# A two-layer diffusion backbone on one Trainium2 core: Q ahead of K, three conditioning sums beside layer 0's experts, and a router on x without its norm

## The chip, the cores and the metric

The kernel runs on one core of one Trainium2 chip. The metric is device time of one execution, in microseconds. The core has TensorE (PE, matmuls; PEld in the profile is its weight load), VectorE (DVE), ScalarE (ACT), GpSimd (POOL) and SyncE (SP), which here only issues DMAs. All weights are float32 and come from HBM once, through one queue of SP.

## What is computed

Two layers on 256 latent tokens and 256 context tokens of width 1024. Cut to what matters here:

```python
mod = silu_c @ ada_w[layer] + ada_b[layer]            # 6 vectors of 1024 for each layer
shift1, scale1, gate1, shift2, scale2, gate2 = split(mod, 6)
h = rmsnorm(x) * (1 + scale1) + shift1
if layer == 0:
    q, k, v, xb, gb = split(h @ w_in)                  # k, v, xb also of the context
    attn = neighbourhood_attention(q, k, v)            # q and k normed by head
    xc = conv4(xb)                                     # depthwise, 4 taps
    y = rglru_forward(xc) + rglru_backward(xc)         # two gated linear scans
    mix = concat(attn, gelu(gb) * y) @ w_out
else:
    mix = real(fft2(h by groups of 256 channels)) @ fnet_w_out
x = x + gate1 * mix
h2 = rmsnorm(x) * (1 + scale2) + shift2
scores = sigmoid(h2 @ router_w)                        # 16 experts, 1 of 4 groups, top 2 in it
x = x + gate2 * sum_over_experts(gates * expert(h2))   # silu(h2 @ Wg) * (h2 @ Wu) @ Wd
```

## The kernel before

**The stream.** Every weight matrix comes in loads of 1 MB into one of 16 slots of SBUF. `Stream` keeps a list of the loads in the order in which they will be used; `pump` issues the next one on SP's queue when a slot is free, and `give`, called by `done` and `used`, frees a slot when its last reader is through. The list is built ahead: the projections of layer 0 in the order of the letters in `ORDER` ("a" is the next ada piece of `ADA`, the letters Q, G, V, o, p the projections, B the attention's bias), then `FILL0`, the eight pairs of layer 0's experts (g, u and d of a pair, four loads each), the two halves of fnet's weights, `GAP` and `FILL1`, then layer 1's experts. An ada piece (l, j) is 512 columns of `ada_w[l]` and fills two slots.

**The ada pieces.** `ada_te` does one piece on TensorE: 64 matmuls with the slot as the stationary operand and the conditioning vector as the moving one, in the tile gv; ACT copies the result (gvr), TensorE turns it, DVE adds the bias into `modc`. In layer 0's front the pieces of `ADA` are interleaved with the projections by the tables `W_K`, `W_Q`, `W_G`, `W_V`; the three pieces of `GAP` run between the last expert of layer 0 and the DFT, `FILL1[0]` in the router of layer 1.

**The front.** Each projection (`gemm`) goes over 8 rows of its weight matrix; a row is split into a high and a low part (ACT makes the high part, DVE or POOL the low one, as the strings `EK`, `EQ`, `EG`, `EV` say: v is DVE, g is POOL) and used in three matmuls (`mm3`, L384 to L386). The order is K, Q, G, V, then attention and `w_out`. Beside them run tasks in pieces: the convolution and the gates of the recurrence beside K, its first scan beside Q and G, the head norms `hk` and `hq` in G and V, the second recurrence beside V. TensorE's order is written out by hand there; that of the other engines is set by a scheduler.

**The norm and the router.** `normed` adds the gated mix to x (gm, xt), sums the squares on ACT and scales x by its norm into xn on DVE. `moe` transposes xn (tp), applies scale and shift to it while it leaves PSUM (h2T), multiplies with the router weights as the stationary operand (lg, four groups of 32 rows), copies that (lr) and folds it with a second product (pick). The selection follows as a chain of small DVE operations (sel, cmp, ..., oh, S); ACT makes xh and POOL xl, the two parts of xn for the gather (xg).

**The experts.** For a pair of experts `up` runs g and u (the gathered tokens stationary, 64 rows for each expert), `transposed_act` at, `down` dn in two halves of 512 columns; the scatter ya of a pair runs inside the next one. The first halves of g, u and dn read two slots, the second halves the other two. In layer 0 the result stays in PSUM and the second norm reads it.

## Time and profile before

| | us |
|---|---|
| median of 3 runs | 792.27 (791.53 to 793.74) |
| profiled execution | 794.38 |
| its span in the trace | 792.6 |
| layer 0's projections, scans, attention | 0 to 248 |
| layer 0's router | 248 to 275.3 |
| layer 0's experts | 275.3 to 490.6 |
| norm, ada pieces, DFT | 490.6 to 523.2 |
| fnet's projection | 523.2 to 546.9 |
| layer 1's router | 546.9 to 571.7 |
| layer 1's experts | 571.7 to 792.6 |

TensorE is busy 89% of the span, DVE 35%, ACT 30%, POOL 16%. The stages are read from TensorE's timeline by the first matmul of each kind. The views that the prediction uses are the slices of the page, the list of waits (for each operation what it waited for last), timelines (one line for a run of like instructions, with the idle time before it in brackets), and groups of instructions by line of the code.

### The profile page before, as it was taken

To read this page: it belongs to the slowest core of one execution; us is meant where nothing else is said; L and a number is where in the kernel's file an instruction comes from. 1 tells how busy PE (TensorE), PEld (TensorE's weight loads), DVE (VectorE), ACT (ScalarE), POOL (GpSimd) and SP (SyncE) were. 2 spreads that over 40 slices of the span, in tenths; PEclk is the share of its full clock that TensorE was granted. 3 is DMA by queue.
4 is the path that set the end of the run, shared out by engine and by line. 5 is a ranking of instruction groups with operands and counts; after the bars stand their busy time and mean duration, and the time that the engine had idled before them with its cause. 6 is when DMAs were issued, how large, how long until landed. Compare 5 with 4: busy or idle time off the path is not lost. (4 is left out here: it accounts for less than half of the span.)

```text
span 792.6 us, 11546 instructions
## 1 busy us (share of the span) xinstructions
PE 708.8 (89%) x4707; PEld 388.6 (49%) x4707; DVE 277.2 (35%) x551; ACT 241.6 (30%) x432; POOL 129.6 (16%) x109
## 2 busy tenths in 40 slices
PE   3999979994997799799999997899699799999996
PEld 2677659563775633343444333667434343344334
DVE  3556388166654511111121104344511111121115
ACT  6233955963665310100110003254310110111001
POOL 1243271363321200000000001032201000000002
PEclk8899998996999899999999999899799999999998
DMA  8989756485656789999999999999299999999995
GB/s 275 356 329 385 311 222 264 167 304 228 265 196 253 296 358 421 416 405 421 421 420 423 418 421 422 420 420 351 112 374 422 417 411 421 421 420 420 423 399 170
DMA packets 53793, 277.41 MB, mean 350 GB/s; under 512 B 4898, under 2 KB 20832, under 8 KB 22496
## 3 DMA queue, kind: packets, MB, share of 16 engines
q1 hardware_dynamic: 53008, 275.95, 87.0%
q8 instruction: 41, 0.67, 0.3%
q10 hardware_dynamic: 720, 0.59, 0.2%
q14 instruction: 24, 0.20, 0.1%
HBM read 275.47 MB, written 1.05 MB: 349 GB/s over the span
## 5 line engine op out<-in xcount | busy, mean ns | idle before, releaser
L1042 PE MATMUL g<-slot,xg 128*64 128x512 f32 x512 | 116.2, 608 | 7.9 <-PEq L1145 7.9
L1079 PE MATMUL dn<-slot,aT 128*64 128x512 f32 (+1 forms) x544 | 114.1, 571 | 3.2 <-DVE aT L1063 3.2
L1042 PE MATMUL u<-slot,xg 128*64 128x512 f32 x512 | 113.0, 592 | 0.0
L372 POOL TENSOR_TENSOR wp<-slot,wp 128x512 fp32r<-128x512 f32 x50 | 68.8, 1385 | 161.6 <-ACT wp L371 161.5
L1042 PEld LDWEIGHTS g<-slot,xg 128*64 128x64 f32 x512 | 38.3, 140 | 81.7 <-issue 80.8
L1048 DVE TENSOR_TENSOR act<-act,u 128x512 f32<-128x512 f32 x16 | 11.0, 687 | 192.1 <-PE u L1042 192.1
L1042 PEld LDWEIGHTS u<-slot,xg 128*64 128x64 f32 x512 | 38.0, 137 | 72.2 <-issue 71.7
L1079 PEld LDWEIGHTS dn<-slot,aT 128*64 128x64 f32 x544 | 37.5, 137 | 68.5 <-issue 60.2
L331 PE MATMUL gv<-slot,sc 128*32 128x128 f32 x1536 | 58.2, 293 | 12.1 <-DMA slot<-in_ada_w_dram 7.7
L1081 ACT ACTIVATE yH<-dn,gcol 128x512 fp32r<-128x512 f32 (+1 forms) x34 | 22.5, 662 | 130.5 <-PE dn L1079 125.3
L997 ACT ACTIVATE xg<-xg,modc,a 128x256 f32<-128x256 f32 x32 | 18.0, 564 | 136.5 <-PE xg L988 136.5
L331 PEld LDWEIGHTS gv<-slot,sc 128*32 128x32 f32 x1536 | 47.8, 118 | 24.0 <-issue 13.0
L999 POOL TENSOR_TENSOR SG<-S,gates 128x512 f32<-128x512 f32 x8 | 8.4, 1044 | 310.5 <-PE st L1051 302.1
L1082 DVE SCALAR_TENSOR_TENSOR yL<-dn,gcol,yH 128x512 fp32r<-128x512 f32 (+1 forms) x34 | 24.4, 719 | 93.6 <-ACT yH L1081 85.4
L371 ACT ACTIVATE wp<-slot 128x512 fp32r<-128x512 f32 x72 | 44.3, 627 | 38.0 <-PE qp L386 11.6
L1047 ACT ACTIVATE act<-g 128x512 f32<-128x512 f32 x16 | 9.6, 597 | 121.4 <-PE g L1042 121.4
L988 PE MATMUL xg<-S,xh 128*128 128x256 f32 x128 | 28.4, 306 | 3.8 <-DVE S L976 2.6
L995 DVE TENSOR_SCALAR xg<-xg,a,modc 128x256 f32<-128x256 f32 x32 | 17.4, 543 | 29.4 <-ACT xg L997 29.4
L988 PE MATMUL xg<-S,xl 128*128 128x256 f32 x128 | 27.4, 298 | 0.0
L1019 PE MATMUL ya<-yH,ST 128*128 128x512 f32 x60 | 26.2, 437 | 0.5 <-ACT yH L1081 0.2
L988 PEld LDWEIGHTS xg<-S,xh 128*128 128x128 f32 x128 | 22.1, 209 | 5.5 <-issue 3.2
L1019 PE MATMUL ya<-yL,ST 128*128 128x512 f32 x60 | 23.9, 399 | 0.9 <-DVE yL L1082 0.9
(252 smaller groups left out, 1047.0 us busy)
## 6 DMA issues: line engine op xcount, KB each, us to landing
slot<-in_moe_g_dram SPq DMA_DIRECT2D x64, 1024.0 KB, 13.5
slot<-in_moe_u_dram SPq DMA_DIRECT2D x64, 1024.0 KB, 15.2
slot<-in_moe_d_dram SPq DMA_DIRECT2D x60, 1024.0 KB, 16.3
slot<-in_ada_w_dram SPq DMA_DIRECT2D x40, 1024.0 KB, 8.3
slot<-in_w_in_dram SPq DMA_DIRECT2D x8, 1024.0 KB, 7.2
slot<-in_ada_w_dram SPq DMA_DIRECT2D x12, 512.0 KB, 9.0
slot<-in_w_out_dram SPq DMA_DIRECT2D x4, 1024.0 KB, 6.3
slot<-in_fnet_w_dram SPq DMA_DIRECT2D x4, 1024.0 KB, 19.8
```

The lines of the kernel that those rows point to most:

```text
L331: te.matmul(out=p[32 * q:32 * q + 32, 0:128], lhsT=sc32[:, k, :], rhs=W[:, k, c:c + 128], start=(k == 0), stop=(k == 7))
L371: ac.activation(dst_h, src, AF.Copy)
L372: eng.tensor_tensor(dst_l, src, dst_h.bitcast(F32), op=ALU.subtract)
L988: at_xg[0] = te.matmul(out=p[:, i * 256:(i + 1) * 256], lhsT=xx[:, tb, k * 128:(k + 1) * 128], rhs=S[:, tb * 256:(tb + 1) * 256], start=(n ...
L995: ve.tensor_scalar(xg[:, k], pv, a2[:, k:k + 1], b2[:, k:k + 1], op0=ALU.mult, op1=ALU.add)
L997: ac.activation(xg[:, k], pv, AF.Identity, scale=a2[:, k:k + 1], bias=b2[:, k:k + 1])
L1019: te.matmul(out=yacc[tb * 2 + h], lhsT=ST[:, tb * 128:(tb + 1) * 128], rhs=y[:, h * 512:(h + 1) * 512], start=(p == 0 and n == 0), stop=(n ...
L1042: te.matmul(out=q[half(i), :], lhsT=xg[:, k, half(i0 + i)], rhs=W[i][:, k], start=(k == 0), stop=(k == 7))
L1048: ve.tensor_tensor(act, act, gu[1], op=ALU.mult)
L1079: te.matmul(out=dn[half(i), :], lhsT=aT[:, fc * 128 + 64 * i:fc * 128 + 64 * i + 64], rhs=W[i][:, fc, c], start=(fc == 0), stop=(fc == 3))
L1081: ac.activation(yH[:, c], dn, AF.Copy, scale=gcol)
L1082: ve.scalar_tensor_tensor(yL[:, c], dn, gcol, yH[:, c].bitcast(F32), op0=ALU.mult, op1=ALU.subtract)
```

## The change

1. Q comes before K in the stream and on TensorE. All of Q's low parts are made on POOL (`EQ`). The convolution now runs beside Q, the gates of the first recurrence and the start of its scan beside K, the rest of the scan beside G, where both head norms begin; the tables are set accordingly. In the attention the recurrence's part of the concatenation and the projection's first step come two steps later.
2. `GAP` is gone. Its three pieces, now `BESIDE`, are loaded behind d of pairs 4, 5 and 6 of layer 0 and summed by `ada_inplace`: eight DVE operations of 128x512 multiply the rows of the piece by the conditioning vector and sum them in place, then four matmuls with one moving column sum over the partitions.
3. `FILL1`'s two pieces run in the second place of layer 1's router, behind the logits, not in the first.
4. `normed` becomes `add_mix`: it gives only the reciprocal r of the norm. The router transposes x itself, its weights carry the scale (w2), the shift becomes a row of biases (crow) from a matmul with ones, and r comes in on DVE behind the product (sc). xh takes r as its scale on ACT; xl is made on DVE, not on POOL. The DFT reads x, and its table carries r (dr).
5. `warm(n)` issues n matmuls of 352 columns whose result nobody reads: 5 in layer 1's router, 3 behind rk in both routers, 8 behind layer 0's experts.

```diff
-FILL1 = [[(1, 10), (1, 11)], [], []]
-GAP = [(1, j) for j in (7, 8, 9)]
-ORDER = 'aaaQaBaaGaaVaapoa'
-EQ = 'vgvgvgvg'
+FILL1 = [[], [(1, 10), (1, 11)], []]
+BESIDE = [(1, j) for j in (7, 8, 9)]
+ORDER = 'aaKaaBaGaaVaaapoa'
+EQ = 'gggggggg'
...
+            if l == 0 and n == "d" and p - 4 in range(len(BESIDE)):
+                r.append(ada_item(*BESIDE[p - 4]))
...
+    def ada_inplace(l, j):
+        W = st.get(("a", l, j))
+        r = W[:, 0]
+        ve.tensor_scalar(r, r, sc32[:, 0, 0:1], None, op0=ALU.mult)
+        for k in range(1, 8):
+            ve.scalar_tensor_tensor(r, W[:, k], sc32[:, k, 0:1], r, op0=ALU.mult, op1=ALU.add)
+        W.done(1)
+        yield
+        p = wps("gv")
+        for q in range(4):
+            te.matmul(out=p[:, q:q + 1], lhsT=r[:, q * 128:(q + 1) * 128], rhs=ones[:, 0:1], start=True, stop=True)
+        c4 = slice(4 * j, 4 * j + 4)
+        ve.tensor_tensor(modc[l][:, c4], p[:, 0:4], ada_b[l][:, c4], op=ALU.add)
+        W.done(0)
+        yield
...
     for n, _ in enumerate(gemm(st.get(("win", WQ)), lambda w, k: rows(qp, w, 2, k), EQ)):
-        scan[0](int(W_Q[1][n]))
-        side(int(W_Q[0][n]))
+        conv(1)
+        side(int(W_Q[n]))
...
+    for n, _ in enumerate(gemm(st.get(("win", WK)), lambda w, k: rows(kp, w, 4, k), EK)):
+        gates[0](int(W_K[1][n]))
+        scan[0](int(W_K[2][n]))
+        side(int(W_K[0][n]))
...
+    def warm(n):
+        p = gps("warm")
+        for _ in range(n):
+            te.matmul(out=p[:, 0:352], lhsT=ones, rhs=cst, start=True, stop=True)
...
+        r = tn([128, 2], "rr", bufs=2)
+        ve.tensor_tensor(r, ss[:, :, 0], ss[:, :, 1], op=ALU.add)
+        ac.activation(r, r, AF.Sqrt, scale=1.0 / D, bias=eps)
+        last = ve.reciprocal(r, r)
...
+        for k in range(8):
+            for tb in range(2):
+                at = te.matmul(out=lv[:, tb], lhsT=xT[:, k, tb * 128:(tb + 1) * 128], rhs=w2[:, k],
+                               start=(k == 0 and tb == 0), stop=(k == 7 and tb == 1))
...
-            gp.tensor_tensor(xl[:, tb], xn[:, tb], xh[:, tb].bitcast(F32), op=ALU.subtract)
+            ac.activation(xh[:, tb], xt[:, tb], AF.Copy, scale=r[:, tb:tb + 1])
+            ve.scalar_tensor_tensor(xl[:, tb], xt[:, tb], r[:, tb:tb + 1], xh[:, tb].bitcast(F32),
+                                    op0=ALU.mult, op1=ALU.subtract)
+        sc = tn([128, 2, NE], "sc")
+        for tb in range(2):
+            ve.scalar_tensor_tensor(sc[:, tb], lv[:, tb], r[:, tb:tb + 1], crow, op0=ALU.mult, op1=ALU.add)
...
                 u = up(p, xg)
+                if l == 0 and p - 5 in range(len(BESIDE)):
+                    next(beside)
...
                 pend = down(u[0], act_t, *u[2:])
+                if l == 0 and p - 4 in range(len(BESIDE)):
+                    beside = ada_inplace(*BESIDE[p - 4])
+                    next(beside)
...
-    fins = [ada_pe(*a, ps_=(gps, wps, wps)[i]) for i, a in enumerate(GAP)]
-    xn, last = normed(yacc, gate, a8("xn", [128, 2, D]))
+    warm(8)
+    r, _ = add_mix(yacc, gate)
+        ve.tensor_scalar(dr[:, tb], dt[:, tb], r[:, tb:tb + 1], None, op0=ALU.mult)
```

What the change moves on the engines, from the order of instructions that each program gives its engines. SP's queue in layer 0's experts, before: the last d loads of pair 6, the DFT's table, the first g load of pair 7.

```order
L128 DMA slot_6632<-in_moe_d_dram 128x2048 [waits DMAHW1_49,PE_49]
L128 DMA slot_6642<-in_moe_d_dram 128x2048 [waits DMAHW2_49,PE_49]
L128 DMA slot_6644<-in_moe_d_dram 128x2048 [waits DMAHW3_49,PE_49]
L123 DMA dft<-in_dft_dram 128x514 [waits DMASW3_49,DMASW7_49,DVE_49,DMAHW4_49,Activation_49,Pool_49]
L128 DMA slot_6710<-in_moe_g_dram 128x2048 [waits DMAHW5_49,PE_49]
```

The same place after: the last d loads of pair 6, then the third ada piece, then g of pair 7.

```order
L129 DMA slot_6738<-in_moe_d_dram 128x2048 [waits DMAHW7_49,PE_49]
L129 DMA slot_6740<-in_moe_d_dram 128x2048 [waits DMAHW0_49,PE_49]
L129 DMA slot_6753<-in_ada_w_dram 128x2048 [waits DMAHW1_49,PE_49]
L129 DMA slot_6755<-in_ada_w_dram 128x2048 [waits DMAHW2_49,PE_49]
L129 DMA slot_6765<-in_moe_g_dram 128x2048 [waits DMAHW3_49,DVE_49]
```

The table went ahead of the last two d loads, and two ada loads came in ahead of pair 7, as two each did behind d of pairs 4 and 5; the load behind a piece waits for DVE.

TensorE at the end of layer 0's experts, before: the last rows of dn of pair 7, the scatter ya, and the first ada piece of the gap (gv).

```order
L1079 MATMUL dn<-slot_6777,aT 64x512
L1019 MATMUL ya<-yH,ST 128x512 [waits Activation_49]
L1019 MATMUL ya<-yL,ST 128x512 [waits DVE_49]
L1019 MATMUL ya<-yH,ST 128x512 [waits Activation_49]
L1019 MATMUL ya<-yL,ST 128x512 [waits DVE_49]
L1019 MATMUL ya<-yH,ST 128x512
L1019 MATMUL ya<-yL,ST 128x512
L1019 MATMUL ya<-yH,ST 128x512
L1019 MATMUL ya<-yL,ST 128x512
L331 MATMUL gv<-slot_6846,sc_127 32x128 [waits DMAHW5_49,PE_49]
L331 MATMUL gv<-slot_6846,sc_127 32x128 x15
L331 MATMUL gv<-slot_6848,sc_127 32x128 [waits DMAHW6_49]
```

After: the middle of dn of pair 7, whose second half reads the last two d loads, to the first row of the scatter.

```order
L1122 MATMUL dn<-slot_6833,aT 64x512
L892 MATMUL warm<-cst 128x352 [waits PE_49]
L1122 MATMUL dn<-slot_6863,aT 64x512 [waits DMAHW5_49]
L892 MATMUL warm<-cst 128x352 x4
L1122 MATMUL dn<-slot_6865,aT 64x512 [waits DMAHW6_49]
L1122 MATMUL dn<-slot_6863,aT 64x512
L1122 MATMUL dn<-slot_6865,aT 64x512
L1122 MATMUL dn<-slot_6863,aT 64x512
L1122 MATMUL dn<-slot_6865,aT 64x512
L1122 MATMUL dn<-slot_6863,aT 64x512
L1122 MATMUL dn<-slot_6865,aT 64x512
L1062 MATMUL ya<-yH,ST 128x512 [waits Activation_49]
```

Five warming matmuls stand inside dn, four of them ahead of the first row that needs the very last load. Three more stand among the scatter's rows, and the DFT follows straight behind it, with no ada piece.

DVE in the front, before, around the evacuation of Q (qr<-qp): Q's last and G's first splits (wp), then the head norms (hs, kq).

```order
L372 TENSOR_TENSOR wp<-slot_945,wp 128x512 [waits DMAHW4_49,Activation_49]
L372 TENSOR_TENSOR wp<-slot_945,wp 128x512 [waits Activation_49]
L594 COPY qr<-qp 128x512 [waits PE_49]
L605 TENSOR_REDUCE hs<-sq 128x8 [waits Activation_49] x5
L372 TENSOR_TENSOR wp<-slot_963,wp 128x512 [waits DMAHW5_49,DVE_49,Activation_49]
L607 RECIPROCAL hs<-hs 128x32 [waits Activation_49]
L605 TENSOR_REDUCE hs<-sq 128x8 [waits Activation_49]
L611 TENSOR_TENSOR kq<-kq,hs 128x512 [waits DVE_49]
L611 TENSOR_TENSOR kq<-kq,hs 128x512 x3
L607 RECIPROCAL hs<-hs 128x16 [waits Activation_49]
L372 TENSOR_TENSOR wp<-slot_963,wp 128x512 [waits Activation_49]
L611 TENSOR_TENSOR qr<-qr,hs 128x512 [waits DVE_49]
```

After, behind the evacuation of K: G's four splits (wp).

```order
L392 TENSOR_TENSOR wp<-slot_834,wp 128x512 [waits DMAHW2_49,Activation_49]
L681 SCALAR_TENSOR_TENSOR A<-A,R 128x512 [waits Activation_49]
L688 SCALAR_TENSOR_TENSOR A<-R,I 128x256 [waits DVE_49,Pool_49]
L392 TENSOR_TENSOR wp<-slot_834,wp 128x512 [waits Activation_49]
L625 TENSOR_REDUCE hs<-sq 128x8 [waits Activation_49]
L682 TENSOR_SCALAR R<-lt 128x512 [waits DVE_49]
L392 TENSOR_TENSOR wp<-slot_852,wp 128x512 [waits DMAHW3_49,Activation_49]
L625 TENSOR_REDUCE hs<-sq 128x8 [waits Activation_49] x2
L690 SCALAR_TENSOR_TENSOR yl<-R,A,I 128x256 [waits DVE_49]
L676 SCALAR_TENSOR_TENSOR lt<-A,R 128x512 [waits DVE_49]
L625 TENSOR_REDUCE hs<-sq 128x8 [waits Activation_49]
L392 TENSOR_TENSOR wp<-slot_852,wp 128x512 [waits Activation_49]
```

Between G's splits stand rows of the first scan (L676 to L690) beside the head norms' sums (hs); before, the scan was over ahead of G and stood among Q's splits.

In layer 1's router DVE's order is now: the first token block's score (sc), the two xl, the second block's score, then sel.

## Rows read from the trace of the kernel before

**Rows 1.** Page, part 2: GB/s moved in each of 40 equal slices of the span.

```profile
GB/s 275 356 329 385 311 222 264 167 304 228 265 196 253 296 358 421 416 405 421 421 420 423 418 421 422 420 420 351 112 374 422 417 411 421 421 420 420 423 399 170
```

**Rows 2.** Waits, TensorE (PE): operation <- releaser: us in total, times, longest us.

```profile
PE gv L339 <- ACT gvr L337: 12.1, 4, 10.2
...
PE gv L331 <- DMA slot<-in_ada_w_dram: 7.7, 4, 5.6
...
PE qp L385 <- DVE wp L372: 4.1, 1, 4.1
...
PE qp L385 <- POOL wp L372: 0.9, 1, 0.9
```

**Rows 3.** Timeline, TensorE, end of layer 0's experts: start us, us, instructions, idle before.

```profile
469.90 7.43 PE L1042 MATMUL u<-slot,xg 128*64 128x512 f32 x32
...
480.44 7.09 PE L1079 MATMUL dn<-slot,aT 128*64 128x512 f32 x32
...
496.15 1.94 PE L331 MATMUL gv<-slot,sc 128*32 128x128 f32 x32 [5.61 <-DMA slot<-in_ada_w_dram]
...
507.12 2.68 PE L1211 MATMUL f<-dft,xn 128*128 128x257 f32 x10
509.73 1.08 PE L331 MATMUL gv<-slot,sc 128*32 128x128 f32 x32
```

**Rows 4.** Timeline, TensorE: g of two successive pairs in layer 1's experts.

```profile
656.62 7.04 PE L1042 MATMUL g<-slot,xg 128*64 128x512 f32 x32
...
682.46 7.04 PE L1042 MATMUL g<-slot,xg 128*64 128x512 f32 x32
```

**Rows 5.** DMA issues, 440 to 520 us: count, KB each, median us to landing.

```profile
slot<-in_moe_d_dram SPq DMA_DIRECT2D x4, 1024.0 KB, 20.1
```

**Rows 6.** Timeline, SP's queue: the issues of pair 7's u and d, layer 0.

```profile
447.89 6.00 SPq L128 DMA_DIRECT2D slot<-in_moe_u_dram  x4
456.04 8.04 SPq L128 DMA_DIRECT2D slot<-in_moe_d_dram  x4
```

**Rows 7.** Groups of instructions by line: count, busy us, mean ns, idle time before and releaser.

```profile
L372 POOL TENSOR_TENSOR wp<-slot,wp 128x512 fp32r<-128x512 f32 x50 | 68.8, 1385 | 161.6 <-ACT wp L371 161.5
...
L372 DVE TENSOR_TENSOR wp<-slot,wp 128x512 fp32r<-128x512 f32 x22 | 17.2, 788 | 19.8 <-ACT wp L371 19.8
...
L577 DVE SCALAR_TENSOR_TENSOR xcT<-xb,cols,xcT 128x512 f32<-128x512 f32 x12 | 10.3, 899 | 0.1
...
L405 PE MATMUL gb<-dg,cst 128*128 128x512 f32 x16 | 7.9, 605 | 0.3 <-POOL dg L400 0.3
```

**Rows 8.** Two windows: busy us (count) of each engine, TensorE's granted clock, DMA share, GB/s.

```profile
280.00:487.00 207.00, 198.14 (x952) 81.17 (x948) 35.23 (x61) 23.04 (x37) 6.92 (x5) 0.99 1.01 418
104.00:118.00 14.00, 8.84 (x36) 6.37 (x35) 14.00 (x13) 5.15 (x10) 10.60 (x7) 0.93 0.52 212
```

**Rows 9.** Timeline, DVE, the norm ahead of the DFT: first sum and last normalization.

```profile
489.89 1.29 DVE L816 TENSOR_TENSOR gm<-ya,gate 128x512 f32<-128x512 f32 x2 [0.82 <-ACT junk L322]
...
498.91 0.75 DVE L417 TENSOR_SCALAR xn<-xt,rs 128x1024 f32<-128x1024 f32 x1
```

**Rows 10.** Timeline, TensorE, the first gather of layer 1's experts, three of its groups.

```profile
566.33 0.63 PE L988 MATMUL xg<-S,xl 128*128 128x256 f32 x2
...
570.15 0.40 PE L988 MATMUL xg<-S,xh 128*128 128x256 f32 x2
...
571.33 0.40 PE L988 MATMUL xg<-S,xl 128*128 128x256 f32 x2
```

**Rows 11.** Timeline, DVE, the selection in layer 1's router.

```profile
558.48 1.09 DVE L920 TENSOR_TENSOR sel<-sc,rb 128x32 f32<-128x32 f32 x1 [0.94 <-ACT sc L907]
559.61 2.36 DVE L925 TENSOR_TENSOR cmp<-sel 128x128 f32<-128x128 f32 x1
562.00 0.29 DVE L927 TENSOR_TENSOR cmp<-cmp,cst 128x128 f32<-128x128 f32 x1
```

**Rows 12.** Timeline, POOL, the same stretch.

```profile
557.18 4.64 POOL L918 TENSOR_TENSOR xl<-xn,xh 128x1024 fp32r<-128x1024 f32 x2 [13.83 <-ACT xh L916]
```

More of the change, by code (lines that the diff above doesn't have):

```diff
@@ L546, in hybrid_layers @@
     st.add([st.chunk(("fw", h), fnet_w[h]) for h in range(2)])
-    st.add([ada_item(*a) for a in GAP + [a for n in FILL1 for a in n]])
+    st.add([ada_item(*a) for n in FILL1 for a in n])
     st.add(exp_items(1))
@@ L679, in hybrid_layers @@
     by_hand.enter_context(tc.manual_schedule(engines={mybir.EngineType.PE}))
-    kp = [acc("kp") for _ in range(4)]
     conv = Task(convolution())
@@ L709, in hybrid_layers @@
         side(int(W_G[0][n]))
-        hk(int(W_G[2][n]))
+        if n == 1:
+            hq(1)
+        if n > 3:
+            hk(1)
     scan[0](99)
+    hk(99)
     evacuate(gb2, [gTf[:, 0:512], gTf[:, 512:1024]])
-    hk(99)
     side(1)
@@ L727, in hybrid_layers @@
             st.give(s_h[2 + n // 4])
+    hq(99)
     scan[1](99)
@@ L884, in moe @@
                 k = 2 * kk + i // 2
[L885 to L892 removed]
+                te.transpose(p[:, i * 128:(i + 1) * 128], xt[:, i % 2, k * 128:(k + 1) * 128], ident)
+            pv = p.rearrange("p (k t) -> p k t", k=2)
+            if kk % 2:
+                ve.tensor_copy(xT[:, 2 * kk:2 * kk + 2], pv)
+            else:
+                ac.activation(xT[:, 2 * kk:2 * kk + 2], pv, AF.Copy)
+        for k in range(8):
+            for tb in range(2):
+                at = te.matmul(out=lv[:, tb], lhsT=xT[:, k, tb * 128:(tb + 1) * 128], rhs=w2[:, k],
+                               start=(k == 0 and tb == 0), stop=(k == 7 and tb == 1))
         for f in fins:
             f()
[L896 to L908 removed]
         with tc.issue_after(at.ins):
@@ L913, in moe @@
         xl = a8("xl", [128, 2, D]).bitcast(F32R)
-        with tc.issue_after(last.ins):
-            for tb in range(2):
-                ac.activation(xh[:, tb], xn[:, tb], AF.Copy)
         for tb in range(2):
-            gp.tensor_tensor(xl[:, tb], xn[:, tb], xh[:, tb].bitcast(F32), op=ALU.subtract)
+            ac.activation(xh[:, tb], xt[:, tb], AF.Copy, scale=r[:, tb:tb + 1])
+            ve.scalar_tensor_tensor(xl[:, tb], xt[:, tb], r[:, tb:tb + 1], xh[:, tb].bitcast(F32),
+                                    op0=ALU.mult, op1=ALU.subtract)
+        sc = tn([128, 2, NE], "sc")
+        for tb in range(2):
+            ve.scalar_tensor_tensor(sc[:, tb], lv[:, tb], r[:, tb:tb + 1], crow, op0=ALU.mult, op1=ALU.add)
+        ac.activation(sc, sc, AF.Sigmoid)
+        table(AF.Silu, sc[:, 0, 0:1])
         sel = tn([128, 2, NE], "sel")
@@ L1192, in hybrid_layers @@
     dts = []
-    xn, _ = normed(mp, gate)
-    yacc, gate = moe(0, xn, False)
-    fins = [ada_pe(*a, ps_=(gps, wps, wps)[i]) for i, a in enumerate(GAP)]
-    xn, last = normed(yacc, gate, a8("xn", [128, 2, D]))
-    with tc.issue_after(last.ins):
-        for f in fins:
-            f()
+    r, _ = add_mix(mp, gate)
+    yacc, gate = moe(0, r, False)
+    warm(8)
+    r, _ = add_mix(yacc, gate)
     dt = dts[0]
+    dr = t2k("dr")[:, 0:514].rearrange("p (t c) -> p t c", t=2)
+    for tb in range(2):
+        ve.tensor_scalar(dr[:, tb], dt[:, tb], r[:, tb:tb + 1], None, op0=ALU.mult)
     a1 = scale_col("a1_1", modc[1], 8, g_mix[1])
@@ L1210, in hybrid_layers @@
         for tb in range(2):
-            te.matmul(out=p[:, 0:257], lhsT=xn[:, tb, cb * 128:(cb + 1) * 128], rhs=dt[:, tb], start=(tb == 0), stop=(tb == 1))
+            te.matmul(out=p[:, 0:257], lhsT=xt[:, tb, cb * 128:(cb + 1) * 128], rhs=dr[:, tb], start=(tb == 0), stop=(tb == 1))
         y = Y[:, cb]
```

96 lines of the change are left out of this document (43 added, 53 removed).

## Prediction, made before the change was run

> **What bounds the kernel now.** I read the page's bandwidth slices first, then the list of what TensorE waited for, then the timelines of the stretches that the change touches. The slices [rows 1] show about 420 GB/s, flat, from 297 to 535 us (slices of 19.8 us): while the first layer's experts run, the one weight stream is never idle. It falls to 112 only in the slice from 555 us, where all 16 slots are full. TensorE's long waits [rows 2] that matter here are few: 10.2 us at the start of the attention, 4.1 for a split of Q's weights, and 5.6 for the first of the late ada pieces [rows 3].
>
> The first layer's experts need the closest look. A pair of experts costs TensorE 25.84 us (656.62 to 682.46, [rows 4]; a pair of layer 1 that waited for no weight). Its 12 MB cost the stream 12 x 2.49 = 29.9 us: with eight loads under way one lands 20.1 us after its issue [rows 5], thus one in 2.5 us, and 1.05 MB at 420 GB/s takes 2.49. So each pair uses up about 4 us of the lead that 16 full slots give at the start. What is left at pair 7? The four u loads of that pair are issued from 447.89 to 453.89 [rows 6], so the last lands at 473.9; TensorE begins u at 469.90 and needs the second half of its slots some 3.6 us later, at 473.5 [rows 3]. The four d loads are issued until 464.08 and the last lands at 484.0; dn begins at 480.44 and needs that slot at about 484. **The lead is zero exactly where the layer ends.** What is put into the stream ahead of these loads delays them one for one, and nothing hides it.
>
> **Part by part.** The profiled execution took 794.4 us (span 792.6); the median of the runs is 792.3. The sums are made on the profile and added to the median.
>
> *The three pieces in the stream.* Six loads of 1 MB stand ahead of the last d loads: 6 x 2.49 = 14.9 us. Pair 5 gets its loads 5 us later with some 8 in hand, so nothing; pair 6 10 later with some 4 in hand; pair 7 14.9 later with none. The last u load lands at 473.9 + 14.9 = 488.8. About half of u remains then, 3.4 us (u takes 7.43, [rows 3]), so u ends at 492.2. From u's end to dn's start passed 3.1 us (477.33 to 480.44). Four one-column matmuls of the last piece and the DVE sums that hang on them now stand in that gap: 1.0 is my choice between 0 and 1.8. dn starts at 496.3 and takes 7.1. Five warming matmuls stand inside dn: one of 512 columns of this type is two records of 0.605 [rows 7], overlapping, so about 0.95, and one of 352 columns about 0.65; 5 x 0.65 = 3.25. dn ends at 506.6 instead of 487.5: **+19.1**. Should the warming matmuls lie in the waits for the last two loads, dn ends at 498.9 (last d landing) + 3.4 = 502.3; 507 is the other end. The DVE chains of the pieces (eight operations of up to 0.90, the two-source row of [rows 7], some 7 us each) lie where DVE is idle: it is busy 35 of 207 us in this phase [rows 8], and each sum must be ready only one projection later. SP now waits for DVE before it reuses a piece's second slot; seven loads are still under way behind it, so that costs nothing.
>
> *What lies between dn and the DFT.* dn ended at 487.5 and the DFT began at 507.12, interrupted for 1.6 us by the last ada piece (1.08 at 509.73 and its turn), so 21.2 us [rows 3]. Without the ada pieces the norm decides. Its DVE chain ran from 489.89 to 499.66 [rows 9]; one normalization of 0.75 falls, two scalings of the DFT table come in, splits of fnet weights move away, and the squares by halves overlap the sums: about 8 us. Ahead of it stand 2.4 us from dn's end, and part of three more warming matmuls, 0.6. From dn to the DFT 11.0: **-10.2**. TensorE stands idle some 7 us of these. After a wait of 6 us the same gather ran at 0.63 first and 0.40 later [rows 10], which is half clock and full: 0 to 2 us, I take 1.0. The region: 19.1 - 10.2 + 1.0 = **+9.9** (4.6 to 11.5).
>
> *Routers.* Off the path go one normalization (0.75), the copy lr (0.42) and the slow forms of sel and cmp: beside POOL's xl [rows 12] they took 1.09 and 2.36, where the next operation of cmp's shape took 0.29 [rows 11]; without POOL about 0.5 for both, so 3.0 less. That is -4.2. Added is xl on DVE, two operations of 1024 columns, 1.29 each as two gm of 512 took [rows 9]. In layer 0 the sigmoid's wait of 0.94 covers part: +1.6. In layer 1 xl stands between the two score operations: +2.6; and there five warming matmuls hold up the last eight logit matmuls, 3.25, two thirds of it under the copies of xT: +1.0. In both, three warming matmuls stand inside the first gather: +1.95. Layer 0 -4.2 + 1.6 + 1.95 = -0.6, and two sums of modulation no longer stand ahead of S, another -0.6: **-1.2** (-4 to +1.5). Layer 1 -4.2 + 2.6 + 1.0 + 1.95 = **+1.3** (-3 to +3.5).
>
> *The front.* Q's stall of 4.1 [rows 2] came of scan work: DVE was busy 14.00 of the 14 us from 104 to 118 [rows 8], and a split of Q stood behind it. Q's splits now run on POOL beside the convolution: -4.1. The scan isn't gone. By DVE's order some 33 instructions, about 26 us at a split's 0.79 [rows 7], now lie between the evacuations of K and of G, with G's four DVE splits among them and V's first behind them; in G before there were some 20, and it had no wait. In proportion to the 14 us that cost 4.1, 26 cost 7.6; V's first two steps need no DVE split and take up some. I take 6.8, nearer the proportion than nothing: **+2.7** (-4 to +7). The wait of 10.2 at the attention stays: ACT's four catH still stand ahead of the exponentials' table load in its order.
>
> In Q all eight splits are now POOL's, at 1.385 each [rows 7]; TensorE's step is six matmuls of 512 columns, 6 x 0.236 = 1.42 by the gather's late pitch [rows 10]. They just match, and I take no wait. The cmp row [rows 11] shows a DVE operation longer beside POOL. The Trainium skill, SBUF — State Buffer ("Who interferes with whom"), says that a DVE instruction with two SBUF inputs contends with a GpSimd instruction that reads SBUF; that speaks for taking xl off POOL and against splitting Q there beside the convolution. The sum without it is the one below; with it, the rival on POOL and Q.
>
> Layer 1's experts start with 16 full slots as before: nothing. Sum: 9.9 - 1.2 + 1.3 + 2.7 = **+12.7**, so 792.3 + 12.7 = **805.0**.
>
> **Rivals.**
> *The stream has room (faster).* If the six loads came without delaying the last d, dn would end only 1.0 later, and the region would give 1.0 - 10.2 = -9.2; with the rest 792.3 - 9.2 + 2.8 = 785.9. It decides from a lead of 15 us at pair 7. Against it: the landing times leave none, and the slices are flat. 0.06.
> *All covers hold (faster).* dn ends at 502.3, the routers give -4 and -3, G hides the scan (-4.1): 792.3 + 4.6 - 11.1 = 785.8. With one of them missing it is 789 to 794, no change that can be measured. 0.06 and 0.09.
> *The warming matmuls hold the clock.* Nine gather groups took 3.82 us (566.33 to 570.15), and five later ones 1.18, 0.42 and 0.24 each [rows 10]. At the later rate from the start each router gets back some 10 x 0.19 = 1.9, and the DFT starts without its 1.0: 805.0 - 4.8 = 800.2. Against it: three of them stand behind the first four gather matmuls. 0.19. The Trainium skill, TensorE: Matmul & The Clock Gate (Part 1), says that the throttled state is the default and activity releases it; the gather's two rates agree, and by that rule this rival is the result.
> *POOL holds Q.* If each of the eight splits waits for one convolution operation of 0.90 [rows 7], 8 x 0.9 = 7.2: 812.2. For it: cmp beside POOL; against it: the longest wait of TensorE for a POOL split was 0.9 [rows 2]. 0.08.
> *G's cover holds alone.* No new stall in the front: 805.0 - 6.8 = 798.2. For it: G had no wait before. 0.12.
>
> **How the numbers follow.** Forecast 0.40 at 805. Faster than 789.9 (0.3%, about what a measurement of this kernel can tell from no change): 0.12; within 0.3%: 0.09; slower 0.79. The range leaves out the faster rivals, and at the top under a tenth: 789 to 814, where 814 is the forecast with the region, the front and layer 1's router near their upper ends.
>
> **What would show it.** Right: waits for moe_u and moe_d loads in TensorE's list, some 10 to 15 us together, in pairs 6 and 7; a DFT that begins about 10 us later after the first expert than before; no wait for ada pieces there; waits for DVE's splits in G and V in place of those in Q; cmp at 0.3. Wrong: no wait for those loads (then the lead was misread), a DFT under 4 us later, or a front that ends over 5 us earlier.

## The result, and the profile after

The changed kernel takes 807.95 us (median; 804.48 to 808.83), the kernel before 793.0 on the same chip: a ratio of 1.0176 with a 95% interval of 1.0154 to 1.0199, or **+14.0 us** (the two medians alone are 15.0 apart). The forecast was 805.0, which is +12.7 on a median of 792.3. The profiled execution of the changed kernel took 808.83, its span is 807.0, against 792.6 before.

By the first TensorE instruction of each kind (fnet's projection by the start of its last matmul) the difference of the two spans, +14.4 us, lies here:

| stage | before | after | difference |
|---|---|---|---|
| to the end of layer 0's `w_out` | 248.00 | 247.35 | -0.65 |
| layer 0's router | 27.28 | 26.92 | -0.36 |
| layer 0's experts, to the end of the last dn | 212.17 | 233.04 | +20.87 |
| last dn to the DFT | 19.67 | 11.39 | -8.28 |
| DFT to the start of fnet's projection | 16.11 | 16.78 | +0.67 |
| fnet's projection | 23.22 | 23.22 | 0 |
| layer 1's router | 25.20 | 26.84 | +1.64 |
| layer 1's experts to the end | 220.95 | 221.46 | +0.51 |

One row of this table can't be read as the price of the change. In layer 1's router the profiled execution of the changed kernel ran part of the time at half clock (1.2 of 2.4 GHz). The same router code ran at full clock throughout in three of the traces below, and took 3.0 us less. The two rows show the whole router in the changed kernel and in the run without the eight warming matmuls, which leaves the router as it is (window and its length, then busy us of TensorE, its loads, DVE, ACT, POOL, then the granted clock).

```profile
558.70:585.50 26.80, 23.17 (x234) 18.45 (x232) 14.01 (x42) 11.71 (x23) 1.05 (x1) 0.87 0.44 173
```

```profile
555.40:579.20 23.80, 20.13 (x234) 16.56 (x232) 14.00 (x42) 11.71 (x23) 1.05 (x1) 1.00 0.49 195
```

The page's slices (20.2 us each here) show the same flat stretch as [rows 1], from the fifteenth on, with one dip to 378. The stream's pause comes earlier than before, in the slices from 504 us: the 16 slots are full while the DFT and fnet's projection run.

```profile
GB/s 280 361 356 403 337 167 130 183 358 212 163 257 344 292 424 421 378 422 421 422 421 421 421 421 421 420 305 156 210 305 422 418 386 423 421 421 421 422 402 181
```

TensorE's list of waits answers to [rows 2] (operation, what ended the wait, us in total, times, longest):

```profile
PE f L1260 <- DVE dr L1251: 7.5, 1, 7.5
PE g L1085 <- DMA slot<-in_moe_g_dram: 5.1, 2, 3.8
...
PE ht L637 <- DVE kq L631: 4.4, 1, 4.4
...
PE u L1085 <- DMA slot<-in_moe_u_dram: 3.9, 4, 1.3
...
PE gbp L406 <- DVE wp L392: 2.5, 2, 1.7
...
PE rk L988 <- DVE oh L984: 1.2, 2, 0.7
...
PE gv L334 <- DMA slot<-in_ada_w_dram: 0.5, 1, 0.5
```

The 5.6 us for the late ada piece is gone, 0.5 remains; the 4.1 for Q's split is gone. New are 5.1 and 3.9 us for expert loads, 7.5 for the table that carries the norm, 4.4 and 2.5 in G of the front. The second router's wait for the one-hot (oh), 6.0 before, is at most 0.7; both routers together wait 1.2. The row of the kernel before:

```profile
PE rk L946 <- DVE oh L942: 7.8, 2, 6.0
```

The timeline of TensorE from g of pair 7 to the DFT (start, us, instructions, idle before) answers to [rows 3]. A reader should look at the idle time in brackets, then at the lengths of the rows that have none.

```profile
471.25 1.12 PE L1085 MATMUL g<-slot,xg 128*64 128x512 f32 x2 [3.76 <-DMA slot<-in_moe_g_dram]
473.73 9.23 PE L1085 MATMUL g<-slot,xg 128*64 128x512 f32 x29 [1.36 <-DMA slot<-in_moe_g_dram]
...
483.67 3.65 PE L1085 MATMUL u<-slot,xg 128*64 128x512 f32 x16 [0.27 <-DMA slot<-in_moe_u_dram]
488.64 3.65 PE L1085 MATMUL u<-slot,xg 128*64 128x512 f32 x14 [1.32 <-DMA slot<-in_moe_u_dram]
...
495.79 3.65 PE L1122 MATMUL dn<-slot,aT 128*64 128x512 f32 x16
499.38 0.86 PE L892 MATMUL warm<-cst 128*128 128x352 f32 x2
500.16 1.07 PE L1122 MATMUL dn<-slot,aT 128*64 128x512 f32 x2
501.17 2.63 PE L892 MATMUL warm<-cst 128*128 128x352 f32 x8
503.73 3.65 PE L1122 MATMUL dn<-slot,aT 128*64 128x512 f32 x14
...
518.70 9.49 PE L1260 MATMUL f<-dr,xt 128*128 128x257 f32 x32 [7.48 <-DVE dr L1251]
```

g waits for its loads, and 29 of its matmuls take 9.23 us where 32 took 7.04 [rows 4]: behind the wait of 3.76 they run at half clock (granted 0.50 from 473 to 478, 1.00 from 480). That costs nothing here, since u waits behind them for its own loads, for the last until 488.64. dn is split in two by five warming matmuls (each two records), 0.86 and 2.63 us long, and ends at 507.31. The DFT follows at 518.70.

### The profile page after: what moved, and what is told of

The parts are those of the page before. It is cut to its first block, busy times and chain, and to the rows that moved or that the text cites. A ratio compares the mean times of both kernels' runs of the same rounds, so it can differ in the third digit from the quotient of the medians.

```text
span 807.0 us, 11360 instructions
## 1 busy us (share of the span) xinstructions
PE 726.8 (90%) x4602; PEld 398.8 (49%) x4602; DVE 291.8 (36%) x577; ACT 243.8 (30%) x435; POOL 124.4 (15%) x107
## 5 line engine op out<-in xcount | busy, mean ns | idle before, releaser
L1085 PE MATMUL g<-slot,xg 128*64 128x512 f32 x512 | 122.2, 627 | 13.3 <-PEq L1193 8.2
L1085 PE MATMUL u<-slot,xg 128*64 128x512 f32 x512 | 115.2, 593 | 3.9 <-DMA slot<-in_moe_u_dram 3.9
L392 POOL TENSOR_TENSOR wp<-slot,wp 128x512 fp32r<-128x512 f32 x52 | 73.5, 1420 | 157.0 <-ACT wp L391 156.9
L334 PE MATMUL gv<-slot,sc 128*32 128x128 f32 x1344 | 51.3, 292 | 4.0 <-ACT sc L307 2.0
L334 PEld LDWEIGHTS gv<-slot,sc 128*32 128x32 f32 x1344 | 42.1, 118 | 14.5 <-issue 7.0
L1031 PE MATMUL xg<-S,xh 128*128 128x256 f32 x128 | 27.3, 295 | 3.3 <-DVE S L1019 2.1
L392 DVE TENSOR_TENSOR wp<-slot,wp 128x512 fp32r<-128x512 f32 x20 | 16.9, 846 | 20.7 <-ACT wp L391 20.5
```

The lines of the kernel that those rows point to most:

```text
L334: te.matmul(out=p[32 * q:32 * q + 32, 0:128], lhsT=sc32[:, k, :], rhs=W[:, k, c:c + 128], start=(k == 0), stop=(k == 7))
L392: eng.tensor_tensor(dst_l, src, dst_h.bitcast(F32), op=ALU.subtract)
L1031: at_xg[0] = te.matmul(out=p[:, i * 256:(i + 1) * 256], lhsT=xx[:, tb, k * 128:(k + 1) * 128], rhs=S[:, tb * 256:(tb + 1) * 256], start=(n ...
L1085: te.matmul(out=q[half(i), :], lhsT=xg[:, k, half(i0 + i)], rhs=W[i][:, k], start=(k == 0), stop=(k == 7))
```

## The experiments

Ratios are to the kernel before on the same chip; microseconds are the ratio times 793. The theory is the prediction's: six loads ahead of the last d loads delay them one for one, since the lead is used up at pair 7; the warming matmuls are plain cost on top; and the gap ahead of the DFT gives some 9 us back. Rivals: SP's queue behind a piece, which waits for DVE; the sums themselves; the front and the routers.

**The pieces back behind fnet's weights.** The three pieces are loaded and summed where they were before, all else is as changed.

```diff
-            if l == 0 and n == "d" and p - 4 in range(len(BESIDE)):
-                r.append(ada_item(*BESIDE[p - 4]))
...
-    st.add([ada_item(*a) for n in FILL1 for a in n])
+    st.add([ada_item(*a) for a in BESIDE + [a for n in FILL1 for a in n]])
...
     warm(8)
-    r, _ = add_mix(yacc, gate)
+    fins = [ada_pe(*a, ps_=(gps, wps, wps)[i]) for i, a in enumerate(BESIDE)]
+    r, last = add_mix(yacc, gate)
...
```

> The changed kernel with one part undone: the three conditioning pieces are again loaded behind fnet's weights and summed by TensorE between layer 0's experts and the DFT; the front, both routers and all warming matmuls stay as changed. Stream theory (six loads ahead of the last d loads delay them one for one): no waits for moe_g and moe_u loads, the last dn ends some 16 us earlier, the DFT waits for ada loads again, 794 to 797 us. Rival (the loss comes of the warming matmuls, the routers or the front): 804 to 809 us.

Measured 796.92, ratio 1.0046 (1.0029 to 1.0062), +3.6 us: 10.4 below the changed kernel, as the stream theory said. TensorE in that run:

```profile
489.08 3.65 PE L1120 MATMUL dn<-slot,aT 128*64 128x512 f32 x14
...
497.13 1.08 PE L332 MATMUL gv<-slot,sc 128*32 128x128 f32 x32 [0.57 <-DMA slot<-in_ada_w_dram]
499.51 1.08 PE L332 MATMUL gv<-slot,sc 128*32 128x128 f32 x32 [1.31 <-DMA slot<-in_ada_w_dram]
503.61 0.37 PE L340 MATMUL gv<-cst,gvr 128*128 128x128 f32 x1 [3.02 <-ACT gvr L338]
...
509.11 2.68 PE L1257 MATMUL f<-dr,xt 128*128 128x257 f32 x10
```

The last dn ends at 492.7 (217.5 us after layer 0's first g, not 233.0), although the same warming matmuls stand in it. The gap then costs most of what it cost before: waits for ada loads (0.57 and 1.31), 3.02 for ACT's copy, and the DFT begins 16.4 us behind dn, not 11.4 (before the change 19.7). 15.6 gained and 5.0 lost come close to the 10.4 of the runs. In the rows of gv the conditioning vector (32 columns) is the stationary operand and the slot the moving one, the other way round than "The ada pieces" says.

**Loads without sums.** The six loads stay in their places; nothing reads them. The eight DVE operations and four matmuls of each piece are left out, and twelve columns of the modulation are set to zero.

```diff
     def ada_inplace(l, j):
...
         W = st.get(("a", l, j))
...
+        ve.memset(modc[l][:, 4 * j:4 * j + 4], 0.0)
         W.done(1)
         yield
...
         W.done(0)
         yield
```

> The changed kernel with the loads of the three pieces left in their places, but without their sums: the eight DVE operations and four matmuls of each are left out and the twelve columns of the modulation set to the bias-free value 0, so the result is another one; SP waits for no DVE chain behind a piece. Stream theory: 805 to 808 us, only the matmuls (about 1 us) and a little of DVE's work in pair 7 go. Rival (queue theory or sums): 794 to 800 us.

Measured 807.22, ratio 1.0164 (1.0142 to 1.0186), +13.0 us. The sums, and the DVE work that SP had to wait for behind a piece, are gone and the time is not. The waits for loads stand where they stood:

```profile
471.05 1.49 PE L1077 MATMUL g<-slot,xg 128*64 128x512 f32 x2 [3.93 <-DMA slot<-in_moe_g_dram]
...
488.44 3.65 PE L1077 MATMUL u<-slot,xg 128*64 128x512 f32 x14 [1.31 <-DMA slot<-in_moe_u_dram]
```

The last row waits for a u load until 488.44; in the changed kernel it was 488.64. By the trace, counted from layer 0's first g, dn ends 0.7 us earlier than in the changed kernel; by the runs the two differ by 1.0, less than their intervals. This speaks against the queue theory and the theory of the sums, which expected 794 to 800.

**One pair earlier.** The pieces stand beside pairs 3, 4 and 5, behind the branch that follows pair 1.

```diff
-            if l == 0 and n == "d" and p - 4 in range(len(BESIDE)):
-                r.append(ada_item(*BESIDE[p - 4]))
+            if l == 0 and n == "d" and p - 3 in range(len(BESIDE)):
+                r.append(ada_item(*BESIDE[p - 3]))
...
```

> The changed kernel with the three pieces one pair earlier, beside pairs 3, 4 and 5: the same six loads ahead of the last d loads, no sum beside pairs 6 and 7, and all sums behind the branch that follows pair 1, which the run with pairs 0 to 2 had its sums ahead of. Stream theory: as the changed kernel less the matmuls and sum in pair 7's gap, 805 to 808 us, with waits for loads of the same size in pairs 6 and 7. Queue theory (SP's wait for DVE late in the layer): 796 to 802 us.

Measured 804.77, ratio 1.0141 (1.0113 to 1.017), +11.2 us. This is 2.8 below the changed kernel, with intervals that overlap, and far from the 796 to 802 of the queue theory. In its trace the DFT begins 0.5 us earlier after layer 0's first g than in the changed kernel; 3.0 us more lie in layer 1's router, which ran at full clock here, and the edit does not touch it. Its waits reach the same end:

```profile
478.54 3.22 PE L1085 MATMUL g<-slot,xg 128*64 128x512 f32 x13 [1.31 <-DMA slot<-in_moe_g_dram]
...
488.49 3.65 PE L1085 MATMUL u<-slot,xg 128*64 128x512 f32 x14 [1.33 <-DMA slot<-in_moe_u_dram]
```

The last u load is there at 488.49, and dn ends at 506.75 (507.31 in the changed kernel), though g of pair 7 never waited more than 1.3 us at a time there and ran at full clock. Six megabytes more ahead of pair 7 move that load by the same time in both places. The pieces also hold two slots each for a while, which no run tries by itself; the slices of the changed kernel's page stay near 420 GB/s through pairs 5 to 7, so there the stream was not short of slots.

**Beside pairs 0 to 2.** Meant as the same test with more distance.

```diff
-            if l == 0 and n == "d" and p - 4 in range(len(BESIDE)):
+            if l == 0 and n == "d" and p in range(len(BESIDE)):
...
```

> The changed kernel with the three pieces loaded and summed beside pairs 0, 1 and 2 of layer 0 instead of 4, 5 and 6: the same six loads ahead of the last d loads, but far from the place where the lead ends. Stream theory: no change, 806 to 810 us, with the same waits for loads in pairs 6 and 7. Rival (queue theory: what costs is SP's wait for DVE behind a piece, or the sums themselves, at pairs 6 and 7 where nothing is in hand): 796 to 802 us.

Measured 815.52, ratio 1.0269 (1.0252 to 1.0286), +21.3 us, 7.3 more than the changed kernel, which neither theory expected. The list of waits has one new entry, and DVE's timeline shows where it comes from:

```profile
PE g L1085 <- DVEq L1193: 21.6, 1, 21.6
```

```profile
343.87 0.49 DVE L376 TENSOR_SCALAR slot<-slot,sc 128x512 f32<-128x512 f32 x1 [17.32 <-DMA slot<-in_ada_w_dram]
...
351.18 1.54 DVE L378 SCALAR_TENSOR_TENSOR slot<-slot,sc,slot 128x512 f32<-128x512 f32 x2 [2.88 <-DVEq L1193]
```

The scheduler had put the third piece's sum ahead of the branch behind pair 1 in DVE's order. DVE stood 17.32 us for the piece's load and reached the branch late, and TensorE waited 21.6 us for DVE at it. So this run is no test of the distance; the run before this one, with all sums behind the branch, is. It shows a second cost of such a sum that the prediction had held for nothing: a queue that works in order must not meet an operand that is not there.

**Without the eight warming matmuls behind the experts, and without any.**

```diff
-    warm(8)
...
-        if not fins:
-            warm(5)
...
-        warm(3)
```

> The changed kernel without the eight warming matmuls behind layer 0's experts. By the trace they take 3.4 us inside the last dn and some 1.4 among the scatter. Theory that they are plain cost: dn ends 3.3 us earlier, 803 to 805 us, the DFT's rate as before. Rival (they keep the clock up for the DFT, or lie in waits that exist anyway): 807 to 810 us.

> The changed kernel without any warming matmul. The run without the eight gave 802.7. By the changed trace the five in layer 1's router hold up its logits by 4.5 us and the three in each first gather take 3.0, and half of that comes back in the gather's rate. Theory that they are mostly cost: 3 for the five and 1.3 for each three, 796 to 798 us. Rival (they pay for themselves by the clock): 801 to 804 us.

Without the eight 802.73, ratio 1.0118 (1.0101 to 1.0134), +9.4; without any 800.3, ratio 1.0078 (1.005 to 1.0106), +6.2 us. So the eight cost 4.6, which is a little more than expected, and all of them 7.8. The run without any came out 2.3 us above the upper end of what was expected of it (1.2 by the ratio). The trace without the eight:

```profile
496.03 7.09 PE L1122 MATMUL dn<-slot,aT 128*64 128x512 f32 x32
...
515.10 9.79 PE L1259 MATMUL f<-dr,xt 128*128 128x257 f32 x32 [8.95 <-DVE dr L1250]
```

dn is whole again and ends at 503.1, and from there to the DFT are 12.0 us; the DFT runs at the same lower rate. By this trace the stretch from layer 0's first g to fnet's projection is 3.6 us shorter than in the changed kernel. In the changed kernel the warming matmuls of layer 1's router look like this:

```profile
564.53 4.79 PE L892 MATMUL warm<-cst 128*128 128x352 f32 x10
569.15 1.85 PE L943 MATMUL lg<-rw,xT 128*128 128x16 f32 x16
...
579.31 2.96 PE L892 MATMUL warm<-cst 128*128 128x352 f32 x6
581.84 0.67 PE L1031 MATMUL xg<-S,xh 128*128 128x256 f32 x2
582.34 0.40 PE L1031 MATMUL xg<-S,xl 128*128 128x256 f32 x2
```

The five hold the last logits up by 4.6 us here, at half clock (granted 0.50 from 564.5 to 567.5), and by 3.1 in the execution at full clock that is shown above. The three in the gather take 2.5 between the groups around them; the gather runs at 0.40 behind them, from its fourth group on instead of the eleventh [rows 10]. From the first group to the first expert it takes 7.25 us, 5.8 in the three executions at full clock, against 5.9 before and 5.3 to 6.7 in the traces of the new router without them. In layer 0 the traces are of one kind: 7.1 to 8.6 us with the three, 5.4 to 5.5 without. There they do raise the rate, and they cost more than the rate returns; in layer 1 that is not shown for the three alone.

**The front of before in the changed kernel.** K ahead of Q, with the tables, head norms and the attention's first steps of before.

```diff
-ORDER = 'aaKaaBaGaaVaaapoa'
-EQ = 'gggggggg'
+ORDER = 'aaaQaBaaGaaVaapoa'
+EQ = 'vgvgvgvg'
...
```

> The changed kernel with the front undone: K before Q, the tables, the head norms and the attention's first steps as before the change; all else as changed. The forecast gave the front +2.7 us; the changed trace shows stalls of 8.6 us there (before 5.3) but the attention begins earlier. If the forecast's term holds, this kernel is 2 to 4 us faster than the changed one: 804 to 806. If the new order saves as much elsewhere as it stalls, as the stage times suggest: 807.5 to 810.

Measured 807.32, ratio 1.0172 (1.0148 to 1.0196), against 1.0176 with the new front: no difference that the intervals can tell. The 2 to 4 us that the forecast's front term promised did not show in the times. They do in the trace: from the first matmul of the first projection to layer 0's first expert TensorE needs 245.4 us here, and 248.2 to 249.4 in the seven traces that have the new front and the same routers. This trace is of the fastest of the run's four executions, so that it settles nothing by itself.

**The pieces ahead of fnet's weights.** The experiments say what a better place must keep: nothing more ahead of the last d loads, and the pieces in the gap before the DFT needs TensorE. In the stream fnet's weights stood between the two, though they are used some 30 us later. So the pieces go behind the last d loads and ahead of fnet's weights, are summed by TensorE in the gap, and the eight warming matmuls go.

```diff
     st.add(exp_items(0))
+    st.add([ada_item(*a) for a in BESIDE])
     st.add([st.chunk(("fw", h), fnet_w[h]) for h in range(2)])
     st.add([ada_item(*a) for n in FILL1 for a in n])
...
```

> The changed kernel with the three pieces loaded behind the last d loads but ahead of fnet's weights, summed by TensorE in its wait for the norm ahead of the DFT, and without the eight warming matmuls. Stream theory: the last dn ends near 487, the pieces land from 486 to 499, the DFT begins at about 499 to 501 instead of 507 before the change, fnet's weights still land ahead of their use: 786 to 790 us. Rival (the pieces in the gap delay the DFT whatever their place in the stream): 793 to 797 us, as the run with the pieces behind fnet's weights.

> The run with the pieces behind the last d loads and ahead of fnet's weights (784.6 us), now without the warming matmuls in the routers too. Between the run without the eight and the one without any, the median fell by some 2.4 us on different chips. If the ones in the routers are cost: 780 to 783 us. If they pay for themselves: 784 to 787.

With the warming matmuls in the routers 784.62, ratio 0.9878 (0.9856 to 0.9901); without them **779.78**, ratio 0.983 (0.9813 to 0.9846), -13.5 us: faster than both kernels. The eleven warming matmuls of the routers cost 3.8 us here, beyond the intervals. TensorE in the faster one, behind the last dn, which ends at 485.9:

```profile
491.40 1.95 PE L332 MATMUL gv<-slot,sc 128*32 128x128 f32 x64
495.28 0.33 PE L340 MATMUL gv<-cst,gvr 128*128 128x128 f32 x1 [1.92 <-ACT gvr L338]
...
496.55 2.68 PE L1254 MATMUL f<-dr,xt 128*128 128x257 f32 x10
```

The first piece is summed among the scatter's rows, the second from 491.40, and the DFT begins at 496.55, 10.7 us behind dn. Its clock stays up, 2.68 us for ten matmuls as in [rows 3], with the pieces ahead of it in place of warming matmuls. That is not so every time: in the trace of the run with the routers' warming matmuls, taken in its slowest execution (791.05), the DFT began at half clock behind the same pieces (granted 0.50 from 499 to 502).

**The same without the new router or front.** The kernel before with the order of the two groups of loads changed, and nothing else.

```diff
-    st.add([st.chunk(("fw", h), fnet_w[h]) for h in range(2)])
-    st.add([ada_item(*a) for a in GAP + [a for n in FILL1 for a in n]])
+    st.add([ada_item(*a) for a in GAP])
+    st.add([st.chunk(("fw", h), fnet_w[h]) for h in range(2)])
+    st.add([ada_item(*a) for n in FILL1 for a in n])
```

> The kernel before with one edit alone: in the stream the three pieces stand ahead of fnet's weights, not behind. Nothing else is changed, the router and the front are those of before. If the pieces' late landing (waits of 5.6, 0.5, 0.9 and 0.8 us in the gap) is what the gap costs, the DFT begins at about 500 instead of 507: 785 to 789 us. If the norm and the router's new form are needed for it: 791 to 794.

Measured 785.22, ratio 0.9913 (0.989 to 0.9936), -6.9 us. In its trace the DFT begins 10.4 us behind the last dn, not 19.7. The waits for ada loads of [rows 2] are down to 1.1, and the old router's wait stays:

```profile
PE rk L947 <- DVE oh L943: 7.8, 2, 6.0
...
PE gv L331 <- DMA slot<-in_ada_w_dram: 1.1, 1, 1.1
```

About half of the best kernel's gain is this one exchange of two loads; the new router without its warming matmuls is, by the traces, the greater part of the rest: in the best kernel's trace layer 1's router takes 22.0 us instead of 25.2, and layer 0's 25.0 instead of 27.3.

**The best kernel with the front of before.**

> As the first run of this set (pieces ahead of fnet's weights, no warming matmuls), with the front of before: K ahead of Q. By the run with the front undone the two orders are worth the same within 2.5 us: between 2 us faster and 2 us slower than the first run of this set. If the forecast's +2.7 for the new front holds, 2 to 4 us faster.

Measured 782.66, ratio 0.9863 (0.9842 to 0.9885), against 0.983 with the new front: 2.6 us slower, with intervals that just overlap, and outside the 2 us that were expected either way. The traces do not put this on the front. With the front of before TensorE needs 245.6 us from its first projection to layer 0's first expert, in the best kernel 247.1. The run loses in layer 1's router, 24.8 us against 21.7, whose code is the same: it ran at half clock from 539.9 to 546.6 here (granted 0.50), and only from 552.1 to 555.4 in the best kernel.

**Sums on DVE beside fnet's projection.** The pieces behind fnet's weights, summed as in the change, but later, no warming matmuls.

```diff
+    sums = [ada_inplace(*a) for a in BESIDE]
+    for s in sums:
+        next(s)
     gate = gate_rows(1, 16)
     for mp in project(fH, fL, lambda h: st.get(("fw", h)), range(8), EF):
         pass
+    for s in sums:
+        next(s)
...
```

> As the run before it, no warming matmuls, but the pieces stay behind fnet's weights in the stream and are summed on DVE beside fnet's projection (eight operations and four matmuls each, as in the change), so that nothing stands between the norm and the DFT. Theory that the gap only needs to be free of late loads: the DFT begins some 11 us after the last dn, at about 497 to 499, at half rate at first; DVE's 20 us of sums lie in the 23 us of the projection among its splits and may hold TensorE up there by 0 to 5: 779 to 787 us.

Measured 792.82, ratio 0.9994 (0.9973 to 1.0015): 5.8 us above the upper end of what was expected. The start went as expected, the DFT at 497.54. But fnet's projection took 3.1 us longer, with DVE's splits behind the sums, and layer 1's router 29.9 us, 7.9 longer than in the best kernel. TensorE there, and then the same stretch of the best kernel:

```profile
540.38 2.73 PE L381 MATMUL gv<-cst,slot 128*128 128x1 f32 x24
...
550.69 3.43 PE L939 MATMUL lg<-rw,xT 128*128 128x16 f32 x16
```

```profile
541.86 1.96 PE L940 MATMUL lg<-rw,xT 128*128 128x16 f32 x16 [0.20 <-ACT xT L937]
```

The twelve column matmuls of the three pieces stand ahead of the transposes for 2.73 us, while DVE waits with x's next sums behind their results; behind that wait the logits run at the lower rate (granted clock 0.50 from 545 to 558.5), 3.43 us for sixteen records that take 1.96 in the best kernel. That the slow rate is all that the router loses beside these 2.73 was not tried.

## Why the prediction was right

The mechanism held: six loads ahead of the last d loads, where the lead is used up, cost what they take in the stream. That the total is so close has luck in it. The forecast gave 9.9 us to the stretch from layer 0's experts to fnet's projection, where 13.3 were measured; 0.1 to the routers, where it was 1.3, in an execution that happened to run layer 1's at half clock; and 2.7 to the front, where it was -0.65. The last error makes up for much of the others.

**The lead at pair 7.** Right, and close. The last u load of pair 7 was put at 488.8; TensorE waited for it until 488.64. u ended at 492.22, as worked out (492.2). The end of dn was put at 506.6 and is 507.31. The term that was too small is that of the five warming matmuls inside dn: dn and they took 11.5 us, where 7.1 and 3.25 were given, and dn alone takes 7.09 in the run without the eight. The slow rows of g had no part in it. Counted from layer 0's first g the stage grew by 20.9, not 19.1, also because that g came 1.0 us earlier and the last load did not. The run with the pieces taken out ends dn at 492.65, 14.7 us earlier, against 14.9 worked out for six loads.

**The cover that was named.** Right in its place, wrong as a rule: DVE's sums beside pairs 4 to 6 cost nothing that the runs can tell (the run without them was 1.0 below, within its interval). Beside pairs 0 to 2 the same sums made TensorE wait 21.6 us at a branch, and the kernel took 7.3 us more. "They lie where DVE is idle" holds only while the operand has landed.

**dn to the DFT.** -10.2 was forecast, with 1.0 for the clock. From dn to the start of fnet's projection the stage moved by -8.3 + 0.7 = -7.6, against -9.2. The wait for the norm was put at 7 us and was 7.48, the whole distance at 11.0 and was 11.39. Two more terms were mis-sized. The last ada piece and its turn held the DFT up by 1.2 us before, by the starts of the rows, where the forecast reckoned 1.6. And the clock cost more: from start to start the DFT's 32 matmuls took 7.5 us before and 9.3 now (granted clock 0.50 from 519 to 523), 1.8, where 0 to 2 had been given and 1.0 taken.

**Routers.** -1.2 and +1.3 were forecast, -0.4 and +1.6 measured. The second is one execution's clock: where the same code ran at full clock the router took 23.8 us, 1.4 less than before the change. sel and cmp did fall, to 0.19 and 0.29 (start, us, DVE; answers to [rows 11]):

```profile
571.19 2.47 DVE L954 SCALAR_TENSOR_TENSOR xl<-xt,rr,xh 128x1024 fp32r<-128x1024 f32 x2
...
574.11 0.19 DVE L962 TENSOR_TENSOR sel<-sc,rb 128x32 f32<-128x32 f32 x1 [0.30 <-ACT sc L959]
574.34 0.29 DVE L967 TENSOR_TENSOR cmp<-sel 128x128 f32<-128x128 f32 x1
```

xl takes 2.47 for both blocks, as worked out from gm. The five warming matmuls of layer 1's router were put at 1.0 and held the logits up by 3.1 to 4.6 us: the copies of xT did not cover two thirds of them, since the last copy ended 0.7 us after the five began.

**The front.** Here both parts of the term were too small. +2.7 was forecast: -4.1 for Q's stall, +6.8 for new ones in G and V. Windows over K and Q together, and over G, before and after (us, then busy us of TensorE, its loads, DVE, ACT, POOL, then the granted clock):

```profile
61.70:124.60 62.90, 57.74 (x568) 40.56 (x566) 39.77 (x52) 37.52 (x57) 26.63 (x18) 0.95 0.74 290
124.60:139.90 15.30, 15.30 (x181) 14.97 (x177) 11.38 (x18) 9.76 (x19) 3.19 (x4) 1.00 0.74 276
```

```profile
60.20:112.60 52.40, 52.40 (x502) 37.02 (x501) 28.50 (x33) 38.08 (x53) 22.11 (x15) 1.00 0.78 311
112.60:138.00 25.40, 17.60 (x181) 16.57 (x178) 25.37 (x32) 14.03 (x27) 15.74 (x10) 0.93 0.45 167
```

The new stalls are as foreseen: 25.40 - 17.60 = 7.8 us in G, for the splits (2.5), the head norm (4.4) and a modulation row (0.9). But G took 10.1 us more in all: its rows were busy 2.3 us longer, at a granted clock of 0.93 in the mean. And K and Q got 10.5 us shorter, not 4.1: their 5.2 us of idle time are gone, the rows behind the old stall no longer run at the lower rate (clock 0.95 to 1.00), and one ada piece less stands there, which costs 1.5 again in the attention. Each part was too small by what a stall drags behind it, and together they make +1.1. (The table has -0.65 mainly because the first projection, which the change leaves alone, began 1.4 us earlier in this execution; it began between 24.7 and 27.0 us in the profiled ones.) Which front is better stays open: the runs show no difference within the changed kernel and 2.6 us for the new one within the best kernel, while by the traces TensorE reaches layer 0's first expert later with the new one in both, the sign that was forecast. (The change also puts three of K's eight splits on DVE instead of one, by `EK`; "The change" does not list it.)

**The rivals.** POOL holding Q did not happen: TensorE was busy 52.40 of 52.40 us in K and Q. But POOL and DVE did hold each other up there. The seven POOL splits beside the convolution, in Q, took 1.68 us in the mean (the row below), and the convolution's two-source operations up to 1.78 us beside them, where they took 0.75 alone. The Trainium skill's page SBUF — State Buffer ("Who interferes with whom") says that a DVE instruction with two SBUF inputs contends with a GpSimd instruction that reads SBUF. The trace agrees.

```profile
L392 POOL TENSOR_TENSOR wp<-slot,wp 128x512 fp32r<-128x512 f32 x7 | 11.7, 1683 | 5.6 <-ACT wp L391 5.6
```

It cost TensorE nothing for a reason that the prediction's step of 1.42 us left out: ada pieces stand between Q's rows, so that its eight rows took 17.6 us, more than eight such splits. The rival in which the warming matmuls hold the clock was half right. The gather ran at 0.40 from its fourth group on. The Trainium skill's page TensorE: Matmul & The Clock Gate (Part 1) has it that activity releases the throttle, and the gather's two rates agree. The kernel lost 7.8 us by them all the same: those inside dn and ahead of the logits stand in TensorE's queue ahead of work that was ready.

## What to carry to other kernels

Work out the lead of a weight stream stage by stage, in loads still to land against work still to do; where it reaches zero, as at pair 7 here, a load put ahead costs its full transfer, and hiding its arithmetic does not help. Order loads by when they are used and by what waits for them at once: exchanging two groups of loads that nobody had weighed against each other was worth 7 us. Taking out the dummy matmuls that were to keep the clock up made the kernel faster in each of the three runs that did it; real work in their place, like the late pieces, kept the DFT at full clock in five of the six traces that have it there. Before pricing a stage from one trace, compare it with the traces of other runs that leave its code alone.

## What the runs showed that was not expected

A branch turns one engine's wait for a load into a wait of another: 17.3 us of DVE became 21.6 of TensorE. A stall of TensorE can cost more than its length, by half clock behind it: the DFT's 32 matmuls behind 7.48 us of waiting took 1.8 us more. Behind 3.76 us of waiting g's matmuls took some 2.8 us more, and that cost nothing, because the next loads were late anyway. And layer 1's router, the same code in eight of the traces, took from 23.8 to 28.3 us, by how long the clock was down in it; what decides that was not found.
